# A one-core hybrid RWKV-7 layer: sample operands loaded at once into a free ring slot, group norm, bonus and state decay written with per-partition scalars

## The chip, the cores and the metric

The kernel runs on one NeuronCore of one Trainium2 chip, in fp32. The metric is device microseconds of one execution. Six engines matter here: PE (TensorE matmul) with its weight loads PEld, DVE (VectorE), ACT (ScalarE), POOL (GpSimd) and SP (SyncE), which here mostly issues DMAs; its queue is called SPq in the profile. The 16 DMA engines of the core move the data.

## The reference, cut to what matters

One decoder layer for 1024 prompt tokens and 64 sample tokens (8 sequences of 8 tokens). One input projection feeds an RWKV-7 time mix (8 heads of 64) and a sliding-window attention; both are gated, concatenated and projected, then a per-layer embedding gate and a last norm follow. The part that the change touches is the time mix and its output:

```
def step(S, inp):
    r_t, w_t, k_t, v_t, kk_t, a_t = inp
    sa = jnp.einsum('bhvk,bhk->bhv', S, kk_t)
    S = (S * w_t[:, :, None, :] - sa[..., None] * (kk_t * a_t)[:, :, None, :]
         + v_t[..., None] * k_t[:, :, None, :])
    return S, jnp.einsum('bhvk,bhk->bhv', S, r_t)
...
yn = (y - mean) * lax.rsqrt(var + GN_EPS) * ln_w.astype(f32).reshape(H, D) + ln_b.astype(f32).reshape(H, D)
bonus = jnp.sum(r * k * r_k.astype(f32).reshape(H, D), axis=-1, keepdims=True) * v
out = (yn + bonus).reshape(B, T, R).astype(z_shift.dtype)
```

It runs over the prompt with a zero state, and over the 8 sample sequences with the state that each brings along.

## The kernel before, in words

The time mix is computed in chunks of 64 tokens: chunks 0 to 15 are the prompt, chunk 16 is the sample. Four chunks form a unit, so units 0 to 3 are the prompt and unit 4 is the sample alone. For each unit `prepare` builds the Gram matrices of the chunk's keys and inverts a triangular matrix; the inversion is a long row of small DVE operations that alternate between two tiles, `tm` and `ti`, each needing the one before. Its result goes out to DRAM (`tt_d`) and comes back in another layout (`B`), is transposed on DVE (`t`) and finished by PE (`TE`, `TF`).

`steps` then carries the state from chunk to chunk. For each chunk, PE computes X1 from the state `sv` (L962), DVE copies it (L964, `rh`), PE computes X2 (L967), ACT and DVE negate it (L968, L969), PE computes X3 (L974), and DVE adds X3 to the decayed state to get the next chunk's `sv`. The decayed state `sg` = `sv` times GC is two POOL operations per chunk, made ahead. Afterwards the output Y of the chunk is made by PE (L987, L990) and normalised by DVE, ACT and POOL. `finish`, once per unit, multiplies each chunk's `y` by the inverse deviation `w` and the weight `lnw` (two POOL operations), multiplies the bonus value `bvl` by the bonus factor `bq` and adds it (two DVE operations), transposes on PE (L942, `ytr`) and stores.

`sample` is unit 4. Here the state differs by sequence, so PE needs the keys masked by sequence. For each head pair p it loads the two halves of the state (`s0`, shown as `s<-in_s0dup`, L1018, two DMAs of 128 KB) and the keys (`kd`, L1021, four DMAs), makes the masked keys `km` (one DVE and one POOL operation per key group), and runs 32 matmuls (L1029, `chS`). The four head pairs share five buffers of tag `y` and two of tag `kd`. DVE then copies `chS` (L1032, `rhS`), PE makes `csS` (L1039, L1044) with unit 4's `B`, and the sample's output is normalised and finished like a chunk.

The operand tiles of a prompt unit (L, two of them, K and B, each 128 partitions by 8 KB) live in two ring slots: slot 0 serves units 0 and 2, slot 1 units 1 and 3. The sample's own operands have a small third slot. Slot 0 is no longer needed once chunk 11, the last of unit 2, has made its Y.

The kernel is built under a tile scheduler: it estimates times and fixes from them the program order of each engine. So an edit also moves instructions that it does not name. Each engine runs its rows in that order; SP's order decides when a DMA can be issued. The stages are written down in a string, `"P0 P1 V0 S0 P2 S1 P3 S2 G4 H0 P4 X4 S3"` (P prepare, V first values, S steps, G gates, H output projection, X the sample). From about 450 us on, the other work that fills PE is the gate projections (`acc_gr`), the attention half of the output projection (`acc_wa`), then the RWKV half (`acc_wr`) and the per-layer gate (`acc_wg`, `pp`) with its row norms.

Of the kernel before, what the change touches and what calls it, by code (L numbers as in the profile page):

```python
# [739 lines left out]
def chain(e):  # L740
    nc, tc, A, O = e.nc, e.tc, e.A, e.O
    V, S, G, PE, SP = e.V, e.S, e.G, e.PE, e.SP
    tt, stt, ts, ps, pool, pc = e.tt, e.stt, e.ts, e.ps, e.pool, e.pc
    MUL, ADD, SUB, MAX = ALU.mult, ALU.add, ALU.subtract, ALU.max
    cst, par, ident, dp = e.cst, e.par, e.ident, e.dp
    kp = e.kp
    early = ("a2", "ti", "tm", "rn", "q2")
    tl = lambda shape, tag, name, bufs: (kp if tag in early else e.kp3 if tag in ("sv", "sg", "rh") else e.kp2).tile(
        shape, F32, tag=tag, name=name, bufs=bufs)
    LO, HI = slice(0, 64), slice(64, 128)  # L750

# [11 lines left out]
    ring = e.ring = {}  # L763
# [135 lines left out]
    def values(ch):  # L899

        q = tl([128, 4, 4, 64], "sv", f"sv{ch}", 2)
        for h, hs in enumerate((HI, LO)):
            DMAQ("sv").dma_start(q[hs, h::2], e.vt_d[ch % 2, ch // 2, h].unsqueeze(1).to_broadcast([64, 2, 4, 64]))
        return q

    def normalise(u, ci, ch, py, un):

        y = tl([128, 4, 64], "y", f"y{ch}", 5)
        mn = tl([128, 4], "mn", f"mn{ch}", 2)
        V.tensor_reduce(mn, py, AX, ADD)  # L910
        ts(G, mn, mn, 1.0 / 64, None, MUL)
        tt(V, y, py, mn.unsqueeze(2).to_broadcast([128, 4, 64]), SUB)
        q = tl([128, 4, 64], "yq", f"yq{ch}", 1)
        S.activation(q, y, AF.Square)
        V.tensor_reduce(un[:, ci], q, AX, ADD)
        return y

    def finish(u, ys, un):
        chs = units[u]
        n = len(chs)  # L920
        w = tl([128, 4, 4], "w", f"w{u}", 2)[:, :n]
        z = tl([128, 4, 4], "z", f"z{u}", 2)[:, :n]
        unv = un[:, :n]
        ts(V, unv, unv, 1.0 / 64, 64e-5, MUL, ADD)
        e.rsqrt(w, unv, z)
        bq = tl([128, 4, 4], "bq", f"bq{u}", 2)[:, :n]
        for b in range(2):
            nb = (n + 1 - b) // 2
            if nb:
                DMAQ("bq").dma_start(bq[:, b::2], e.bon_d[b, chs[0] // 2:chs[0] // 2 + nb].rearrange("c h t p -> (h t) c p"))  # L930
        for ci, ch in enumerate(chs):
            c, cl = src(ch)
            y = ys[ci]
            tt(G, y, y, w[:, ci].unsqueeze(2).to_broadcast([128, 4, 64]), MUL)
            tt(G, y, y, lnw, MUL)
            bv = tl([128, 4, 64], "bv", f"bvl{ch}", 2)
            DMAQ("bvl").dma_start(bv, e.vt_d[ch % 2, ch // 2].rearrange("h t p v -> (h t) p v"))
            tt(V, bv, bv, bq[:, ci].unsqueeze(2).to_broadcast([128, 4, 64]), MUL)
            tt(V, y, y, bv, ADD)
            t = ps("tr", f"ytr{ch}", 1)[:, 0:256].rearrange("p (a b) -> p a b", a=4)  # L940
            for q in range(2):
                PE.transpose(t[:, 2 * q:2 * q + 2].rearrange("p a b -> p (a b)"),  # L942
                             y[:, 2 * q:2 * q + 2].rearrange("p a b -> p (a b)"), ident)
            orr = tl([128, 4, 64], "or", f"or{ch}", 1)
            S.copy(orr, t)
            DMAQ("or").dma_start(e.or_d[c][:, :, 64 * cl:64 * cl + 64], orr)

    def steps(u, r, sv, last):
        chs = units[u]
        un = tl([128, 4, 4], "un", f"un{u}", 2)  # L950
        ys = []
        for ci, ch in enumerate(chs):
            L, K = r.L[ci], r.K[ci]
            pch = ps("ch", f"ch{ch}", 2).rearrange("p (a b) -> p a b", a=8)
            X1, X2 = pch[:, 0:4], pch[:, 4:8]
            sg = tl([128, 4, 64], "sg", f"sg{ch}", 2)
            for h, hs in enumerate((LO, HI)):
                tt(G, sg[hs], sv[hs, h], e.GC[hs, ch].unsqueeze(2).to_broadcast([64, 4, 64]), MUL)
            with tc.high_priority():
                for p in range(4):  # L960
                    for h, hs in enumerate((LO, HI)):
                        PE.matmul(X1[hs, p], L[h][:, p, 0:64], sv[:, h, p], start=True, stop=True)  # L962
                rh = tl([128, 4, 64], "rh", f"rh{ch}", 2)
                V.tensor_copy(rh, X1)  # L964
                for p in range(4):
                    for h, hs in enumerate((LO, HI)):
                        PE.matmul(X2[hs, p], r.B[hs, ci, p, 0:64], rh[hs, p], start=True, stop=True)  # L967
                S.activation(sv[LO, 2], X2[LO], AF.Copy, scale=-1.0)  # L968
                V.tensor_scalar(sv[HI, 3], X2[HI], -1.0, None, MUL)  # L969
                p3 = ps("ch", f"cs{ch}", 2).rearrange("p (a b) -> p a b", a=8)  # L970
                X3, Y = p3[:, 0:4], p3[:, 4:8]
                for p in range(4):
                    for h, hs in enumerate((LO, HI)):
                        PE.matmul(X3[hs, p], K[:, p, 64 * h:64 * h + 64], sv[:, 2 + h, p], start=True, stop=True)  # L974
                if ch < 15:
                    nx = values(ch + 1)
                    for h, hs in enumerate((LO, HI)):
                        tt(V, nx[hs, h], X3[hs], sg[hs], ADD)
                else:
                    so = tl([128, 4, 64], "rh", "so", 2)  # L980
                    tt(V, so, X3, sg, ADD)
                    SP.dma_start(O["wkvp"], so)
                    nx = None

            for p in range(4):
                for h, hs in enumerate((LO, HI)):
                    PE.matmul(Y[hs, p], L[h][:, p, 64:128], sv[:, h, p], start=p == 0, stop=False, skip_group_check=True)  # L987
            for p in range(4):
                for h, hs in enumerate((LO, HI)):
                    PE.matmul(Y[hs, p], r.B[hs, ci, p, 64:128], sv[hs, 2 + h, p], start=False, stop=True, skip_group_check=True)  # L990
            ys.append(normalise(u, ci, ch, Y, un))
            sv = nx
            e.fill(("s", u))
        finish(u, ys, un)
        return sv

    def sample(r):
        u, ch = 4, 16
# [3 lines left out]
        sv = tl([128, 2, 4, 64], "svS", "svS", 1)  # L1002
# [4 lines left out]
        mb = e.bm[:, :256].rearrange("p (b t) -> p b t", b=4)  # L1007
        for p in range(4):
            for q, dst in ((0, X1), (1, Y)):
                for h, hs in enumerate((LO, HI)):  # L1010
                    os_ = HI if h == 0 else LO
                    PE.matmul(dst[hs, p], L[h][os_, p, 64 * q:64 * q + 64], sv[os_, h, p], start=p + q == 0,
                              stop=False, skip_group_check=True)
        for p in range(4):
            s0, kd = [], []
            for h, hs in enumerate((LO, HI)):
                s0.append(tl([128, 4, 64], "y", f"s0{p}{h}", 5))
                DMAQ("s0").dma_start(s0[h], A["s0dup"][:, :, p, h])  # L1018
                kd.append(tl([128, 2, 64], "kd", f"kd{p}{h}", 2))
                for x in (LO, HI):  # L1020
                    DMAQ("s0").dma_start(kd[h][x], e.kq_d[16, hs, p].rearrange("k (s t) -> k s t", s=2))  # L1021
            for q, dst in ((0, X1), (1, Y)):
                km = []
                for h in range(2):
                    km.append(tl([128, 4, 64], "y", f"km{p}{h}{q}", 5))
                    tt(G if h else V, km[h], kd[h][:, q].unsqueeze(1).to_broadcast([128, 4, 64]), mb, MUL)
                for b in range(4):
                    for h, hs in enumerate((LO, HI)):
                        PE.matmul(dst[hs, p], km[h][:, b], s0[h][:, b], start=False, stop=b == 3, skip_group_check=True)  # L1029
            yield  # L1030
        rh = tl([128, 4, 64], "y", "rhS", 5)
        V.tensor_copy(rh, X1)  # L1032
# [13 lines left out]
        un = tl([128, 4, 4], "un", "unS", 2)  # L1046
        y = normalise(u, 0, ch, yy, un)
        finish(u, [y], un)
        yield
        b2 = e.bm[:, 256:].unsqueeze(2).to_broadcast([128, 8, 64])  # L1050
# [17 lines left out]
    for o in ORDER.split():  # L1068
        u = int(o[1])
        if o[0] == "V":  # L1070
            lnw = e.lnw = e.kp2.tile([128, 4, 64], F32, name="lnw")
# [4 lines left out]
            sv = values(0)  # L1076
# [11 lines left out]
        elif o[0] == "S":  # L1088
            sv = steps(u, rs[u], sv, 0)
# [414 lines left out]
```

## Time and profile before

| | |
|---|---|
| median of three runs | 960.12 us (959.53 to 960.18) |
| the profiled execution's own time | 954.67 us |
| its span, first to last instruction | 952.9 us |
| mean granted TensorE clock | 0.925 of full speed |
| PE busy | 837.2 us, 88% |
| PEld busy | 742.5 us, 78% |
| DVE busy | 640.8 us, 67%, 1511 instructions |
| ACT busy | 373.6 us, 39% |
| POOL busy | 371.8 us, 39%, 494 instructions |

The profiled execution is 5.45 us shorter than the median. Its span is what the trace's times count from; 1.8 us of the execution lie outside the span. Busy shares are averages over stages with different limits, so the table by windows of 50 us is the one to read. PEclk there is the granted clock as a share of full speed, and a busy PE at 0.70 does less than one at 1.00.

### The profile page before, as it was taken

To read this page: it belongs to the slowest core of one execution; us is meant where nothing else is said; L and a number is where in the kernel's file an instruction comes from. 1 tells how busy PE (TensorE), PEld (TensorE's weight loads), DVE (VectorE), ACT (ScalarE), POOL (GpSimd) and SP (SyncE) were. 2 spreads that over 40 slices of the span, in tenths; PEclk is the share of its full clock that TensorE was granted. 3 is DMA by queue.
4 is the path that set the end of the run, shared out by engine and by line. 5 is a ranking of instruction groups with operands and counts; after the bars stand their busy time and mean duration, and the time that the engine had idled before them with its cause. 6 is when DMAs were issued, how large, how long until landed. Compare 5 with 4: busy or idle time off the path is not lost.

```text
span 952.9 us, 17528 instructions
## 1 busy us (share of the span) xinstructions
PE 837.2 (88%) x6352; PEld 742.5 (78%) x6352; DVE 640.8 (67%) x1511; ACT 373.6 (39%) x864; POOL 371.8 (39%) x494
## 2 busy tenths in 40 slices
PE   6978999999999989898899875998893699999994
PEld 4878999788886779787788764887773588899993
DVE  7856487777777443388855778597963686864464
ACT  6202086666756432742233343313431144322131
POOL 7538466665667222323321333133442254301000
PEclk9989899999999999899899965998976799999997
DMA  8013201322226338546544597777657289998882
GB/s 288 23 64 96 65 23 56 101 91 71 69 90 176 84 83 220 162 104 164 149 131 132 139 306 231 179 259 188 204 171 230 69 280 334 335 308 289 267 295 99
DMA packets 151047, 157.81 MB, mean 166 GB/s; under 512 B 63688, under 2 KB 121288, under 8 KB 150824
## 3 DMA queue, kind: packets, MB, share of 16 engines
q1 hardware_dynamic: 150144, 155.57, 54.1%
q10 hardware_dynamic: 816, 1.11, 0.4%
q8 instruction: 50, 0.82, 0.4%
q14 instruction: 37, 0.30, 0.1%
HBM read 106.77 MB, written 49.67 MB: 164 GB/s over the span
## 4 chain that ended last, share of the span: by engine, by line
PE 40%; DVE 26%; DMA 15%; ACT 6%; issue 6%; SPq 4%; POOL 2%; DVEq 0%; ACTq 0%; POOLq 0%
PE acc_z L157 6%; PE acc_gr L157 4%; DVE tm L55 3%; PE acc_q L157 2%; DVE ti L55 2%; ACT s L425 2%; PE ov L446 2%; PE pp L1346 2%; DVE xl L58 2%; DMA a<-at_d 2%; PE acc_wg0g L157 1%; DMA sg<-sg_d 1%; DMA kd<-kq_d 1%; DMA L<-kq_d 1%; PE acc_wg4g L157 1%
## 5 line engine op out<-in xcount | busy, mean ns | idle before, releaser
L157 PE MATMUL acc_z<-xh,wh_z 128*128 128x384 f32 (+1 forms) x312 | 64.8, 339 | 0.0
L157 PE MATMUL acc_z<-xl,wh_z 128*128 128x384 f32 (+1 forms) x312 | 63.1, 333 | 0.0
L157 PE MATMUL acc_z<-xh,wl_z 128*128 128x384 f32 (+1 forms) x312 | 62.5, 331 | 0.0
L55 DVE TENSOR_TENSOR tm<-a,ti 128x56 f32<-128x56 f32 (+28 forms) x152 | 55.1, 362 | 3.6
L157 PEld LDWEIGHTS acc_z<-xh,wh_z 128*128 128x128 f32 x312 | 53.3, 190 | 1.7 <-ACT pTS L505 0.2
L157 PEld LDWEIGHTS acc_z<-xl,wh_z 128*128 128x128 f32 x312 | 53.1, 190 | 0.5
L157 PEld LDWEIGHTS acc_z<-xh,wl_z 128*128 128x128 f32 x312 | 52.3, 188 | 1.0 <-issue 0.2
L55 DVE TENSOR_TENSOR ti<-ti,tm 128x56 f32<-128x56 f32 (+28 forms) x152 | 48.1, 316 | 3.5
L55 POOL TENSOR_TENSOR sg<-sv,GC 64x256 f32<-64x256 f32 x32 | 21.5, 672 | 59.8 <-DVE sv L55 47.4
L64 POOL TENSOR_SCALAR s<-s,sm 128x256 f32<-128x256 f32 (+1 forms) x64 | 34.8, 560 | 17.2 <-ACT pT L444 4.6
L1185 ACT ACTIVATE q<-hx 128x384 f32<-128x384 f32 (+1 forms) x41 | 20.8, 507 | 48.8 <-DVE hx L58 20.8
L800 PE MATMUL gram<-L,K 64*128 64x128 f32 x272 | 31.6, 327 | 5.9 <-issue 4.0
L55 POOL TENSOR_TENSOR wl_z<-wr_z,wh_z 128x1024 fp32r<-128x1024 f32 x13 | 31.3, 2405 | 10.8 <-ACT wh_z L146 4.8
L800 PEld LDWEIGHTS gram<-L,K 64*128 64x128 f32 x272 | 27.0, 222 | 10.5 <-issue 7.5
L55 DVE TENSOR_TENSOR sq<-sq,q 128x384 f32<-128x384 f32 (+1 forms) x41 | 25.6, 624 | 13.1 <-ACT q L1185 12.4
L55 DVE TENSOR_TENSOR zr<-acc_z,R 128x384 f32<-128x384 f32 (+2 forms) x52 | 21.7, 433 | 18.5 <-PE acc_z L157 18.2
L425 ACT ACTIVATE s<-s,sm 128x256 f32<-128x256 f32 (+1 forms) x64 | 30.9, 485 | 1.9 <-DVE sm L62 1.9
L446 PE MATMUL ov<-pT,vtok 128*64 128x512 f32 x60 | 30.9, 633 | 0.4 <-ACT pT L444 0.4
L1356 ACT ACTIVATE t<-t 128x384 f32<-128x384 f32 (+3 forms) x25 | 12.2, 494 | 45.5 <-DVE t L55 45.4
L804 ACT COPY B<-L 64x512 f32<-64x512 f32 x34 | 20.9, 616 | 21.8 <-DVE L L55 20.9
L62 POOL TENSOR_SCALAR mn<-mn 128x4 f32<-128x4 f32 x17 | 4.4, 262 | 63.9 <-DVE mn L910 58.8
L55 DVE TENSOR_TENSOR L<-gram,cst 128x512 f32<-128x512 f32 x34 | 22.5, 684 | 8.7 <-PE gram L800 8.5
(620 smaller groups left out, 2458.4 us busy)
## 6 DMA issues: line engine op xcount, KB each, us to landing
wr_z<-in_wz SPq DMA_DIRECT2D x13, 512.0 KB
L<-kq_d SPq DMA_DIRECT2D x24, 256.0 KB
sv<-vt_d SPq DMA_DIRECT2D x32, 128.0 KB
wh_wo<-wo_dh SPq DMA_DIRECT2D x8, 512.0 KB
wl_wo<-wo_dl SPq DMA_DIRECT2D x8, 512.0 KB
raw<-in_xT SPq DMA_DIRECT2D x8, 384.0 KB
kq_d<-KQ SPq DMA_DIRECT2D x8, 384.0 KB
bk_d<-BK SPq DMA_DIRECT2D x8, 384.0 KB
```

The costliest lines, as they stand in the source:

```text
L55: e.tensor_tensor(out, a, b, op=op)
L58: V.scalar_tensor_tensor(out, a, s, b, op0, op1)
L62: e.tensor_scalar(out, a, s1, None, op0)
L64: e.tensor_scalar(out, a, s1, s2, op0, op1)
L157: PE.matmul(acc[:, :n], w_[:, k0 + k, :], a_[c][:, k, :n], start=i + k == 0, stop=i == 2 and k == K - 1)
L425: S.activation(s[:, j, :nk], s[:, j, :nk], AF.Exp, bias=m[:, 0, j:j + 1], accum_out=m[:, 2, j:j + 1])
L446: PE.matmul(ov[own, :], vtok[:, blk, own], pT[g].rearrange("p a b -> p (a b)"), start=pos == 0, stop=pos == nb - 1)
L800: PE.matmul(Gp[h][:, p], bk[hs, p], L[h][hs, p], start=True, stop=True)
L804: S.copy(r.B[hs, ci], L[h][hs])
L1185: e.S.square(q, h)
L1346: PE.matmul(pa, w[:, i], p[:, i], start=i + j == 0, stop=i == 1 and j == len(pr) - 1)
L1356: S.activation(t, t, AF.Tanh, scale=0.5)
```

## The change

Three edits. In `steps`, the two POOL operations for `sg` and the two DVE additions of 64 x 256 become eight DVE operations of 64 partitions x 64 elements that multiply the state by one GC value per partition and add X3 in the same pass. In `finish`, the two POOL and two DVE operations of 128 x 256 per chunk become eight DVE operations of 128 x 64: `y` times `w` times `lnw`, and `bv` times `bq` plus `y`. In `sample`, the state is one DMA of 1 MB into the first L tile of ring slot 0, the keys are four DMAs into the second, and all sixteen `km` are made at once in its K tile (DVE) and B tile (POOL), before one block of 128 `chS` matmuls.

```diff
-    tl = lambda shape, tag, name, bufs: (kp if tag in early else e.kp3 if tag in ("sv", "sg", "rh") else e.kp2).tile(
+    tl = lambda shape, tag, name, bufs: (kp if tag in early else e.kp3 if tag in ("sv", "rh") else e.kp2).tile(
...
-            tt(G, y, y, w[:, ci].unsqueeze(2).to_broadcast([128, 4, 64]), MUL)
-            tt(G, y, y, lnw, MUL)
             bv = tl([128, 4, 64], "bv", f"bvl{ch}", 2)
             DMAQ("bvl").dma_start(bv, e.vt_d[ch % 2, ch // 2].rearrange("h t p v -> (h t) p v"))
-            tt(V, bv, bv, bq[:, ci].unsqueeze(2).to_broadcast([128, 4, 64]), MUL)
-            tt(V, y, y, bv, ADD)
+            for p in range(4):
+                stt(y[:, p], y[:, p], w[:, ci, p:p + 1], lnw[:, p], MUL, MUL)
+            for p in range(4):
+                stt(y[:, p], bv[:, p], bq[:, ci, p:p + 1], y[:, p], MUL, ADD)
...
-            sg = tl([128, 4, 64], "sg", f"sg{ch}", 2)
-            for h, hs in enumerate((LO, HI)):
-                tt(G, sg[hs], sv[hs, h], e.GC[hs, ch].unsqueeze(2).to_broadcast([64, 4, 64]), MUL)
...
                 if ch < 15:
                     nx = values(ch + 1)
-                    for h, hs in enumerate((LO, HI)):
-                        tt(V, nx[hs, h], X3[hs], sg[hs], ADD)
+                    new = lambda h, hs: nx[hs, h]
                 else:
                     so = tl([128, 4, 64], "rh", "so", 2)
-                    tt(V, so, X3, sg, ADD)
+                    new = lambda h, hs: so[hs]
+                for p in range(4):
+                    for h, hs in enumerate((LO, HI)):
+                        stt(new(h, hs)[:, p], sv[hs, h, p], e.GC[hs, ch, p:p + 1], X3[hs, p], MUL, ADD)
+                if ch == 15:
                     SP.dma_start(O["wkvp"], so)
...
+        RS, RD, RM = ring[0][0], ring[0][1], ring[0][2:]
+        s0 = RS.rearrange("p c q d -> p (c q d)").rearrange("p (b q h v) -> p b q h v", b=4, q=4, h=2)
+        kd = RD.rearrange("p c q d -> p (c q d)")[:, :1024].rearrange("p (h q d) -> p h q d", h=2, q=4)
+        km = [x.rearrange("p c q d -> p (c q d)").rearrange("p (q s b t) -> p q s b t", q=4, s=2, b=4) for x in RM]
+        DMAQ("s0").dma_start(s0, A["s0dup"])
+        for h, hs in enumerate((LO, HI)):
+            for x in (LO, HI):
+                DMAQ("s0").dma_start(kd[x, h], e.kq_d[16, hs])
         for p in range(4):
-            s0, kd = [], []
-            for h, hs in enumerate((LO, HI)):
-                s0.append(tl([128, 4, 64], "y", f"s0{p}{h}", 5))
-                DMAQ("s0").dma_start(s0[h], A["s0dup"][:, :, p, h])
-                kd.append(tl([128, 2, 64], "kd", f"kd{p}{h}", 2))
-                for x in (LO, HI):
-                    DMAQ("s0").dma_start(kd[h][x], e.kq_d[16, hs, p].rearrange("k (s t) -> k s t", s=2))
+            for h in range(2):
+                for q in range(2):
+                    tt(G if h else V, km[h][:, p, q], kd[:, h, p, 64 * q:64 * q + 64].unsqueeze(1).to_broadcast([128, 4, 64]), mb, MUL)
+        for p in range(4):
             for q, dst in ((0, X1), (1, Y)):
-                km = []
-                for h in range(2):
-                    km.append(tl([128, 4, 64], "y", f"km{p}{h}{q}", 5))
-                    tt(G if h else V, km[h], kd[h][:, q].unsqueeze(1).to_broadcast([128, 4, 64]), mb, MUL)
                 for b in range(4):
                     for h, hs in enumerate((LO, HI)):
-                        PE.matmul(dst[hs, p], km[h][:, b], s0[h][:, b], start=False, stop=b == 3, skip_group_check=True)
+                        PE.matmul(dst[hs, p], km[h][:, p, q, b], s0[:, b, p, h], start=False, stop=b == 3, skip_group_check=True)
```

The scheduler moves more than the diff shows. SP's queue before, around the second and third head pair's loads (`s<-in_s0dup` is the state, `kd` the keys; the other rows are stores and weights):

```order
357 L1018 DMA s_7021<-in_s0dup 128x4x64
358 L946 DMA or_d_3665<-or_5973 512x1x64
359 L1021 DMA kd_7023<-kq_d 64x128 x2
360 L1021 DMA kd_7028<-kq_d 64x128
361 L1018 DMA s_7026<-in_s0dup 128x4x64
362 L1021 DMA kd_7028<-kq_d 64x128
363 L1302 DMA wg_dl<-wl_wg1g_8176 128x1024
364 L1152 DMA or_8050<-or_d_3665 128x768
365 L1153 DMA sg_8051<-sg_d_3659 128x768
```

And SP's queue now, around the one load of the state (L1019, into the L tile `L_3687`; `sv_7252` are the values of chunk 13):

```order
336 L1304 DMA wo_dl<-wl_wor6c_8040 128x2x512
337 L1272 DMA wl_wor0c_8154<-wo_dl 128x2x512
338 L143 DMA wr_wg1g_8239<-in_wg 128x1024
339 L1019 DMA L_3687<-in_s0dup 128x2048
340 L903 DMA sv_7252<-vt_d 64x2x256 x2
341 L1304 DMA wg_dh<-wh_wg0g_8178 128x1024
```

The sample's loads no longer lie between the stores of unit 2's outputs and the weights of the gate stage; the state's load stands ahead of the values of chunk 13, and the keys' loads 13 to 30 rows ahead of it.

DVE before, near the end of unit 4's triangular inversion (`ti_6869`, `tm_6874`), with the next state `sv` of chunk 14 and the additions of unit 2's outputs `y`:

```order
1083 L55 TENSOR_TENSOR ti_6869<-ti_6869,tm_6874 64x2x3
1084 L55 TENSOR_TENSOR y_5717<-y_5717,bvl_5930 128x256
1085 L55 TENSOR_TENSOR tm_6874<-a_4_6853,ti_6869 64x4
1086 L55 TENSOR_TENSOR sq_7832<-sq_7832,q_7993 128x384
1087 L55 TENSOR_TENSOR ti_6869<-ti_6869,tm_6874 64x4
1088 L58 SCALAR_TENSOR_TENSOR ul_7831<-hx_6823,par,uh_7830 128x384
1089 L55 TENSOR_TENSOR y_5779<-y_5779,bvl_5942 128x256
1090 L55 TENSOR_TENSOR hx_6823<-acc_wr7c_0_7998,hx_6823 128x384
1091 L55 TENSOR_TENSOR sv_7280<-cs_7271,sg_7248 64x256 x2
```

The same stretch of DVE now (`ti_6953`, `tm_6958` are the inversion's tiles, `rhS` the copy of the sample's `chS`, `rsv` and `rsy` a row norm):

```order
1111 L55 TENSOR_TENSOR ti_6953<-ti_6953,tm_6958 64x2x3
1112 L1034 COPY rhS<-chS 128x256
1113 L64 TENSOR_SCALAR rsv_8084<-st_8083 128x3
1114 L55 TENSOR_TENSOR tm_6958<-a_4_6937,ti_6953 64x4
1115 L58 SCALAR_TENSOR_TENSOR y_5906<-bvl_6028,bq_5993,y_5906 128x64 x4
1116 L62 TENSOR_SCALAR rsy_8085<-rsv_8084 128x3
1117 L55 TENSOR_TENSOR ti_6953<-ti_6953,tm_6958 64x4
1118 L58 SCALAR_TENSOR_TENSOR y_5971<-bvl_6044,bq_5993,y_5971 128x64 x4
1119 L55 TENSOR_TENSOR tm_6958<-a_4_6937,ti_6953 64x7
1120 L64 TENSOR_SCALAR rsy_8085<-rsy_8085 128x3
1121 L55 TENSOR_TENSOR ti_6953<-ti_6953,tm_6958 64x7
1122 L55 TENSOR_TENSOR rsq_8086<-rsy_8085 128x3
```

The inversion of unit 4 used to end ahead of everything that reads the sample's `chS`; now its last rows stand behind `rhS`, most of those behind the new `sv` of chunk 14 as well (row 1123, eight operations), and the last `ti` is row 1144. On PE the 128 matmuls of `chS` now stand as one block, after chunk 12's X3 and before `acc_wg0g`, with X1 and X2 of chunk 13 among them; before, they were spread from `acc_wg0g` to `csS`.

## Rows read from the trace of the kernel before

**Rows 1.** Windows of 50 us: length, busy of each engine, granted clock, DMA share, GB/s.

```profile
550.00:600.00 50.00, 33.98 (x260) 29.31 (x261) 40.73 (x109) 20.29 (x45) 18.31 (x26) 0.65 0.87 258
600.00:650.00 50.00, 45.83 (x532) 41.12 (x530) 39.26 (x104) 13.73 (x23) 12.51 (x14) 0.97 0.77 227
650.00:700.00 50.00, 41.03 (x515) 34.74 (x515) 44.43 (x129) 18.49 (x35) 24.78 (x23) 0.84 0.63 187
700.00:750.00 50.00, 30.78 (x333) 24.97 (x332) 24.89 (x61) 9.31 (x21) 13.78 (x18) 0.70 0.54 162
...
800.00:850.00 50.00, 49.29 (x287) 44.43 (x284) 38.40 (x89) 15.80 (x33) 13.52 (x13) 1.00 0.95 323
```

**Rows 2.** Groups of instructions by line, 450 to 760 us: busy, mean ns, idle before.

```profile
L1029 PE MATMUL chS<-s,km 128*64 128x64 f32 x128 | 8.9, 276 | 13.3 <-DVE km L55 9.7 <-POOL km L55 3.5
```

**Rows 3.** Timeline of PE, 681 to 755 us: start, length, what, idle before and releaser.

```profile
681.07 0.68 PE L990 MATMUL cs<-sv,B 64*64 64x64 f32 x16
...
698.07 2.91 PE L157 MATMUL acc_wg0g<-uh,wh_wg0g 128*128 128x384 f32 x8
...
732.05 1.70 PE L1029 MATMUL chS<-s,km 128*64 128x64 f32 x18 [4.41 <-DVE km L55]
...
736.20 1.21 PE L1039 MATMUL csS<-rhS,B 64*64 64x64 f32 x16 [0.68 <-DVE rhS L1032]
...
741.75 1.12 PE L962 MATMUL ch<-sv,L 128*64 128x64 f32 x16 [2.28 <-DVE y L55]
...
754.20 0.97 PE L157 MATMUL acc_wr0c<-mrh,wh_wor0c 128*128 128x384 f32 x4
```

**Rows 4.** The chain that ended last, 700 to 745 us, in order of time.

```profile
714.19 6.76 DMA wh_wor2c<-wo_dh
...
724.75 6.00 DMA kd<-kq_d
```

**Rows 5.** Timeline of DVE: end of unit 4's inversion, and its return from DRAM.

```profile
691.63 0.15 DVE L55 TENSOR_TENSOR ti<-ti,tm 64x4 f32<-64x4 f32 x1
...
701.81 0.30 DVE L879 STREAM_TRANSPOSE t<-B 32x128 f32<-32x128 f32 x1 [0.76 <-DMA B<-tt_d]
```

**Rows 6.** Instructions of tile sg: ns min/median/max, first and last start.

```profile
L55 POOL TENSOR_TENSOR sg<-sv,GC x32: 605/610/1671, 459.1 to 748.5; 64x256 f32<-64x256 f32 x32
L55 DVE TENSOR_TENSOR sv<-cs,sg x30: 404/422/429, 479.8 to 747.6; 64x256 f32<-64x256 f32 x30
```

**Rows 7.** Tile zsr: an existing form with a per-partition scalar, down to 128x64.

```profile
L58 DVE SCALAR_TENSOR_TENSOR zsr<-zr,par,zsr x16: 272/559/1256, 149.7 to 285.0; 128x384 f32<-128x384 f32 x8, 128x256 f32<-128x256 f32 x4, 128x64 f32<-128x64 f32 x4
```

**Rows 8.** Timeline of DVE, 279 and 683 us: independent operations that follow each other.

```profile
279.15 0.21 DVE L55 TENSOR_TENSOR zr<-acc_z,R 128x64 f32<-128x64 f32 x1
279.29 0.69 DVE L58 SCALAR_TENSOR_TENSOR zsr<-zr,par,zsr 128x384 f32<-128x384 f32 x1
...
683.17 0.15 DVE L55 TENSOR_TENSOR tm<-a,ti 64x4 f32<-64x4 f32 x1
683.24 0.16 DVE L58 SCALAR_TENSOR_TENSOR z<-z,un 128x16 f32<-128x16 f32 x1
```

**Rows 9.** Instructions of tile y, columns as in rows 6.

```profile
L55 POOL TENSOR_TENSOR y<-y,w x17: 608/613/1060, 529.5 to 770.4; 128x256 f32<-128x256 f32 x17
L55 POOL TENSOR_TENSOR y<-y,lnw x17: 721/727/2460, 531.8 to 775.8; 128x256 f32<-128x256 f32 x17
L55 DVE TENSOR_TENSOR y<-y,bvl x17: 407/418/949, 532.6 to 781.4; 128x256 f32<-128x256 f32 x17
```

**Rows 10.** Timelines of DVE and POOL, 583 to 589 us: the inversion of unit 2.

```profile
583.48 0.23 DVE L55 TENSOR_TENSOR tm<-a,ti 128x70 f32<-128x70 f32 x1
583.74 0.56 DVE L55 TENSOR_TENSOR ti<-ti,tm 128x70 f32<-128x70 f32 x1
...
588.05 0.63 DVE L55 TENSOR_TENSOR tm<-a,ti 128x16 f32<-128x16 f32 x1
...
583.61 2.33 POOL L55 TENSOR_TENSOR y<-y,w 128x256 f32<-128x256 f32 x4 [7.53 <-DVE w L58]
```

## The prediction

> **What bounds the kernel now.** The windows of 50 us come first [rows 1]. PE is the bound at 800 to 850 us (49.3 of 50 us busy at full clock), but not from 550 to 750 us: there it idles 16.0, 4.2, 9.0 and 19.2 us, and its clock is low in the first window (0.65) and the last (0.70). The last is the weakest stretch of this half of the kernel: DVE has only 24.9 us of work in it, POOL 13.8, and the DMA share is 0.54. So nothing is full; things wait for each other. The groups of instructions say what [rows 2]: the 128 `chS` matmuls of the sample work 8.9 us and PE stands 13.3 us in front of them, for `km` on DVE and POOL. The timeline of PE gives the places [rows 3], such as 4.41 us before 732.05. Behind the last `chS` come `csS` at 736.20, X1 of chunk 14 at 741.75 and only at 754.20 `acc_wr0c`, the first large work in which PE is full again. The chain that ended last shows why `km` is late [rows 4]: it goes through a load of keys, of 32 KB, that needs 6.00 us to land, behind a weight load of 512 KB that needs 6.76 us; each is issued when a shared buffer comes free. The sample's loads are therefore a chain of buffers and DMA round trips, on the path that sets the end.
>
> **The change, part by part.**
>
> **The sample's loads.** Eight state loads and sixteen key loads become one and four, and sixteen `km` can be made as soon as the keys are there, which SP issues well ahead. The wait of 13.3 us for `km` [rows 2] goes. What is late next is the state: its slot is free when chunk 11 has made Y, which ended at 681.75 us [rows 3]. The trace has no load of 1 MB. The nearest rows are 6.00 us (32 KB) and 6.76 us (512 KB) [rows 4]: lower bound 6, upper bound twice the second, 13.5. These two differ little for sixteen times the bytes, so I take 8. With about 2 us of lateness of chunk 11 (below) and 1 us to issue, the state lands at about 693. Then 128 matmuls, at 0.07 us each as in the row of 18 in 1.70 us, or 9 us at the low clock [rows 3], with some of chunk 13's between: the block ends near 702 instead of 735.
>
> **What stands behind the block.** `acc_wg0g`, 698.07 us before [rows 3], now follows it, at about 702, and ends near 707 with chunk 13's X3 behind. On DVE, unit 4's inversion, which ended at 691.63 before [rows 5], now ends behind `rhS` and the new `sv` of chunk 14, so near 711: this is the new late one. From its last `ti` to the transpose `t` it takes 10.2 us (691.63 to 701.81 [rows 5]), two DMA trips that the change leaves alone: `t` at about 721, covered on PE by `acc_wg1g` and `pp`. `TE` and `TF` I put at 2.5 us, an estimate from the 1 us that 16 to 18 small matmuls take [rows 3], twice, and a copy; then `csS` at 724. From `csS` to X1 of chunk 14 took 5.55 us (736.20 to 741.75 [rows 3]); it comes at 729.6, so 12.1 us earlier.
>
> **State decay.** 32 POOL operations of 0.61 us (median) go, 21 us in all with the longer ones; none was waited for at the chunk step, so POOL's relief is worth nothing by itself [rows 6]. On DVE two additions of 0.42 us become eight operations of 64 elements. The nearest form in the trace, with a per-partition scalar and 128 x 64, takes 0.272 us at the least [rows 7]; that is the upper bound of what each costs in a row: 2.2 us. The lower is the pitch of independent operations of 4 elements: 683.17 to 683.24, 0.07 us, so 0.7 us [rows 8]. One of 128 x 64 with duration 0.21 lets the next start after 0.14 (279.15 to 279.29): an overlap of 0.07. I take 0.272 less 0.07, so 0.20, and 1.7 us for eight: plus 0.85 us per chunk, 14 us over 16 chunks (bounds minus 2 and plus 22). It lies directly on the chain from chunk to chunk.
>
> **Group norm and bonus.** Two DVE operations of 0.42 us become eight of 0.20: plus 0.85 us per chunk, 14.5 us over 17 chunks (bounds minus 2.5 and plus 23). Two POOL operations of 0.61 and 0.73 us per chunk go, 23 us [rows 9]. There is a gain in them on DVE: beside POOL's `y` of unit 1, from 583.61 us on, `ti` and `tm` take 0.56 to 0.63 us where the one before takes 0.23 [rows 10]. Nine operations run there, at about 0.35 us each: 3.2 us, which nearly pays for that unit's 3.4 us. The same holds beside unit 2's four chunks.
>
> A rule of the Trainium skill stands against both edits. In "VectorE: DVE Perf Modes", section "The TRN2 errata — SBUF-src ops pay a fixed extra latency per instruction", it says that a vector operation pays a fixed latency, so that many small tiles pay it many times, and it advises tiles of 512 elements or more. By its measured fixed term of about 150 cycles an operation of 64 elements is estimated at 0.22 us, and the two edits together at 31 us of DVE work instead of my 28.5. For the old additions of 256 elements the same term would give 0.42 us, and the row agrees (418 ns [rows 9]). No run here shows the new forms yet.
>
> **Sum.** From 550 us to chunk 11's Y: four state updates and unit 1's finish cost 3.4 us each, less the 3.2 us of stall; most of the rest lies in DVE's idle time (25.6 of the 150 us from 550 to 700 are idle [rows 1]) or under the `acc_wa` matmuls. I take plus 2, the lateness used above. To X1 of chunk 14: minus 12.1, with that in it. One more state update to chunk 15, plus 0.85, and `acc_wr0c` comes 11.2 us earlier, at 743. Behind it the finishes of unit 3 and the sample add 5 x 0.85 = 4.3 us on DVE, less a stall of some 1.5, partly under PE's work: plus 2. The rest, in which PE is full, moves as it is: **minus 9 us**. Against the profiled execution of 954.67 us that gives 945.7. The median of the runs stands 5.45 us above that execution, so the forecast in its terms is **951 us**.
>
> **The rivals.**
> *Unit 4's inversion does not hold back.* If DVE reaches its last rows as early as PE allows, `csS` follows `acc_wg1g` directly, at about 716, and the clock stays up in the block: 8 us more, 943. For it: DVE had 25 us of idle time in that stretch. Against: the order puts the last `ti` behind `sv`, which waits for X3 behind `acc_wg0g`.
> *The edit does not free the loads.* The one load is all or nothing: if it takes the 13.5 us of the upper bound, PE stands in front of the block, with nothing of the queue behind it movable ahead, and 5.5 us are lost; chunk 13's values and the stores of `wg_dh` are queued behind it on SP. With the DMA engines at 0.95 in 800 to 850 us [rows 1], weights that now are wanted earlier may not come earlier and take the rest: 958 to 961, no change.
> *VectorE becomes the bound* (the other side). The mechanism: no overlap between the small operations, so plus 1.4 us per update and per finish, in line in the chunk chain and in the inversions of units 2 and 4. From chunk 4 to 15 that is 12 updates and 8 finishes, 28 us, less 7 of stalls; against the 25.6 us of idle time, which is scattered, I reckon that all 21 come through, less the 12 won at the sample: 969 us, plus 9. It decides where the price of an operation passes 0.25 us or where the inversion, not PE, ends last in each unit. That is also where the skill's rule points. For it: PE idles 16 us in 550 to 600 us, when DVE is busiest (40.7). Against: the stalls that POOL causes there go with the same edit.
>
> **How the numbers follow.** Forecast 0.52 (947 to 956); inversion early 0.15; loads not freed 0.14; VectorE bound 0.19. A measurement of this kernel can tell about 0.2%, here 1.9 us. Faster by over 0.2%: all of the first two but 0.02, and 0.05 of the third: 0.70. Within: 0.02 of the first and 0.08 of the third, and 0.02 of the fourth: 0.12. Slower: 0.17 of the fourth and 0.01 of the third: 0.18. The range reaches from the early inversion to the middle of the cases of a loss: 940 to 965.
>
> **What would show it.** In the profile after: `chS` as one stretch with no wait for `km`, and one wait of 1 to 5 us for the DMA of the state before it; `acc_wg0g` at about 702, X1 of chunk 14 at about 730, `acc_wr0c` at about 743; rows of 64 x 64 and 128 x 64 on DVE with eight in about 1.7 us; `ti` and `tm` of unit 2 without the 0.5 us durations around finish; POOL busy some 45 us less, DVE 10 to 20 us more; PEclk of the 700 to 750 window above 0.70. Wrong would be: the small operations at 0.28 us each in a row; chunk 8's steps more than 4 us later than before; the state landing after 697; a wait of PE for `TE` that ends after 725; or DMA waits in 760 to 840 us that take back what the sample won.

## The result and the profile after

The change makes the kernel **slower**: 969.95 us (968.62 to 974.23, four runs) against 959.83 us (four runs) for the kernel before, a ratio of 1.0118 with a 95% interval of 1.0082 to 1.0154. The forecast was 951 us. Of all the executions behind this document one, of 985.62 us (e10), fell in a slower state of the chip, and the ratios leave it out.

| | before | after |
|---|---|---|
| median of the runs | 959.83 us | 969.95 us |
| the profiled execution | 954.67 us | 974.23 us |
| its span | 952.9 us | 972.4 us |
| DVE busy | 640.8 us, x1511 | 664.0 us, x1710 |
| POOL busy | 371.8 us, x494 | 326.4 us, x428 |

One caution holds for the whole of what follows: the profiled execution before lies 5.2 us under its median and the one after 4.3 us over it, so the two traces differ by 19.6 us where the runs differ by 10.1. Places are read from the traces, sizes from the runs. In one place the trace shows where its execution lost time: from 500 to 513 us PE is busy throughout, but the granted clock is 0.51 of full speed, the lower of its two levels (1.2 of 2.4 GHz). X2 of chunk 2, 16 matmuls, takes 1.12 us there. In the kernel before it takes 0.68 us, at a clock of 1.00. In the 8 us up to 496, before its clock fell, PE had been busy 6.97 us. The windows, with the columns of [rows 1], are first that of the changed kernel and then that of the kernel before:

```profile
500.00:513.00 13.00, 13.00 (x146) 11.02 (x148) 3.05 (x7) 2.38 (x5) 0.22 (x1) 0.51 0.27 63
```

```profile
494.00:504.00 10.00, 10.00 (x173) 8.76 (x174) 4.33 (x10) 3.11 (x7) 2.03 (x4) 1.00 0.57 165
```

The page of the changed kernel, its part 1:

```profile
PE 850.8 (87%) x6352; PEld 754.5 (78%) x6352; DVE 664.0 (68%) x1710; ACT 374.0 (38%) x864; POOL 326.4 (34%) x428
```

POOL lost 45 us, as forecast, and DVE gained 23 us (forecast 10 to 20). The windows after, with the columns of [rows 1]:

```profile
550.00:600.00 50.00, 35.02 (x326) 27.03 (x325) 43.08 (x143) 17.09 (x39) 7.56 (x8) 0.74 0.94 273
600.00:650.00 50.00, 46.03 (x451) 41.73 (x451) 36.96 (x107) 17.02 (x31) 12.21 (x13) 0.88 0.77 224
650.00:700.00 50.00, 40.54 (x499) 34.71 (x498) 44.12 (x116) 18.54 (x33) 19.89 (x20) 0.93 0.72 227
700.00:750.00 50.00, 32.54 (x412) 27.76 (x412) 34.19 (x142) 11.35 (x25) 5.77 (x6) 0.74 0.48 149
750.00:800.00 50.00, 37.02 (x260) 33.65 (x261) 39.45 (x112) 14.28 (x29) 11.62 (x10) 0.75 0.57 190
```

The last of these windows in the kernel before, for comparison:

```profile
750.00:800.00 50.00, 43.42 (x280) 38.19 (x279) 36.61 (x64) 19.89 (x38) 22.25 (x20) 0.94 0.76 253
```

The weak stretch of 700 to 750 us has not gone; a second one, 750 to 800 us at 0.75 of full clock (0.94 before), stands behind it. The next fence is the groups of instructions from 450 to 780 us, as in [rows 2]:

```profile
L58 DVE SCALAR_TENSOR_TENSOR sv<-sv,GC,cs 64x64 f32<-64x64 f32 x120 | 33.6, 280 | 5.4 <-PE cs L971 2.0
...
L58 DVE SCALAR_TENSOR_TENSOR y<-bvl,bq,y 128x64 f32<-128x64 f32 x52 | 12.8, 287 | 0.5 <-DMA bvl<-vt_d 0.4
L58 DVE SCALAR_TENSOR_TENSOR y<-y,w,lnw 128x64 f32<-128x64 f32 x52 | 11.9, 281 | 0.0
...
L1031 PE MATMUL chS<-L,K 128*64 128x64 f32 x64 | 6.2, 266 | 0.0
L1031 PE MATMUL chS<-L,B 128*64 128x64 f32 x64 | 6.2, 266 | 0.0
```

The sample's edit does what it says: the 128 `chS` matmuls now wait for nothing (0.0 where 13.3 us stood). What is late is ahead of them and behind them. The timeline of PE after, answering to [rows 3]; the first row is Y of chunk 11, the second chunk 12's X2, the third chunk 12's X3 just ahead of the block, the last two X1 of chunk 14 and the first `acc_wr0c` behind it:

```profile
694.05 0.68 PE L990 MATMUL cs<-sv,B 64*64 64x64 f32 x16
...
696.91 0.68 PE L964 MATMUL ch<-rh,B 64*64 64x64 f32 x16 [1.23 <-DVE rh L961]
701.64 0.45 PE L971 MATMUL cs<-sv,K 128*64 128x64 f32 x2 [3.16 <-DVE ti L55]
...
738.53 0.97 PE L1041 MATMUL csS<-rhS,B 64*64 64x64 f32 x16 [0.37 <-ACT B L894]
...
748.29 1.12 PE L959 MATMUL ch<-sv,L 128*64 128x64 f32 x16 [7.18 <-DVE y L55]
...
766.37 1.65 PE L157 MATMUL acc_wr0c<-mrh,wh_wor0c 128*128 128x384 f32 x4
```

Which row of the kernel before answers to the first has to be counted, since the rows carry no chunk numbers. X3 of chunk 15 is the last at 753.58 us, and counted back from it these are X3 of chunk 11, Y of chunk 11 and X3 of chunk 12:

```profile
658.74 0.48 PE L974 MATMUL cs<-sv,K 128*64 128x64 f32 x2
...
666.65 0.68 PE L990 MATMUL cs<-sv,B 64*64 64x64 f32 x16
...
673.87 0.69 PE L974 MATMUL cs<-sv,K 128*64 128x64 f32 x16
```

So the Y at 681.07 in [rows 3] is that of chunk 12, and chunk 11's Y, at 694.05 us, comes 27.4 us later than before. The lateness came in steps: X3 is 1.6 us late in chunk 1, 10.8 in chunk 2 (the stretch at the low clock, where X1 of chunk 2 is also spread over 7.3 us between other matmuls, against 2.9 before), 11.1 in chunk 7, 20.1 in chunk 8, behind unit 2's inversion, and 27.3 in chunk 11. The timeline of DVE has the end of unit 4's inversion and its return, answering to [rows 5]:

```profile
725.15 0.15 DVE L55 TENSOR_TENSOR ti<-ti,tm 64x4 f32<-64x4 f32 x1
...
732.89 0.30 DVE L879 STREAM_TRANSPOSE t<-B 32x128 f32<-32x128 f32 x1 [1.38 <-DMA B<-tt_d]
```

The inversion ends 33.5 us later than before, and with it `B`, the last thing that `csS` waits for. One more wait follows, on DVE again:

```profile
744.01 1.15 DVE L58 SCALAR_TENSOR_TENSOR or<-or,lnb,sg 128x384 f32<-128x384 f32 x2 [2.43 <-DMA sg<-sg_d]
745.07 0.41 DVE L910 TENSOR_REDUCE mn<-yS 128x4 f32<-128x256 f32 x1
```

A row of the output projection that waits for a DMA stands on DVE ahead of the normalisation; X1 of chunk 14, whose row names the normalisation's `y`, comes 9.8 us after `csS` where it was 5.55.

### The profile page after: what moved, and what is told of

Same layout as the page of the kernel before. It is cut to its first block, busy times and chain, and to the rows that moved or that the text cites. A ratio compares the mean times of both kernels' runs of the same rounds, so it can differ in the third digit from the quotient of the medians.

```text
span 972.4 us, 17568 instructions
## 1 busy us (share of the span) xinstructions
PE 850.8 (87%) x6352; PEld 754.5 (78%) x6352; DVE 664.0 (68%) x1710; ACT 374.0 (38%) x864; POOL 326.4 (34%) x428
## 4 chain that ended last, share of the span: by engine, by line
PE 43%; DVE 26%; DMA 12%; issue 7%; ACT 7%; SPq 3%; POOL 2%; DVEq 0%; ACTq 0%; POOLq 0%
PE acc_z L157 6%; DVE tm L55 3%; PE acc_gr L157 3%; PE acc_wa L157 2%; DVE ti L55 2%; PE acc_q L157 2%; PE pp L1348 2%; ACT s L425 2%; DVE y L58 2%; PE ov L446 2%; PE acc_wg3g L157 2%; DVE sv L58 2%; PE acc_wg0g L157 1%; PE acc_wg7g L157 1%; PE acc_wg5g L157 1%
## 5 line engine op out<-in xcount | busy, mean ns | idle before, releaser
L55 DVE TENSOR_TENSOR tm<-a,ti 128x56 f32<-128x56 f32 (+28 forms) x152 | 52.9, 348 | 2.9
L58 DVE SCALAR_TENSOR_TENSOR sv<-sv,GC,cs 64x64 f32<-64x64 f32 x120 | 33.6, 280 | 5.4 <-PE cs L971 2.0
L959 PE MATMUL ch<-sv,L 128*64 128x64 f32 x256 | 22.3, 261 | 12.8 <-DVE y L55 7.2
L959 PEld LDWEIGHTS ch<-sv,L 128*64 128x64 f32 x256 | 16.6, 159 | 20.2 <-DVE y L55 7.3
```

The lines of the kernel that those rows point to most:

```text
L55: e.tensor_tensor(out, a, b, op=op)
L58: V.scalar_tensor_tensor(out, a, s, b, op0, op1)
```

## The experiments

Two theories for the loss were set against each other, with a third against both. A: the state decay costs the time, in the chain from chunk to chunk. B: the norm's small operations cost it, in the inversions. C: the sample's block costs it. The three edits were taken apart and recombined. "Ratio" is to the kernel before on the same chip, with a 95% interval.

**e1, the sample alone.** The change without its edits of `steps` and `finish`:

```diff
+            sg = tl([128, 4, 64], "sg", f"sg{ch}", 2)
+            for h, hs in enumerate((LO, HI)):
+                tt(G, sg[hs], sv[hs, h], e.GC[hs, ch].unsqueeze(2).to_broadcast([64, 4, 64]), MUL)
...
-                for p in range(4):
-                    for h, hs in enumerate((LO, HI)):
-                        stt(new(h, hs)[:, p], sv[hs, h, p], e.GC[hs, ch, p:p + 1], X3[hs, p], MUL, ADD)
...
-            for p in range(4):
-                stt(y[:, p], y[:, p], w[:, ci, p:p + 1], lnw[:, p], MUL, MUL)
+            tt(G, y, y, w[:, ci].unsqueeze(2).to_broadcast([128, 4, 64]), MUL)
...
```

> Only the sample's loads are changed; state decay and group norm are as before. Theory A (the state decay in eight small operations costs the time: 2.46 us for eight in the changed kernel's trace against 0.87 for two, in the chain from chunk to chunk) and theory B (the group norm's small operations among the inversion's cost it): the gain of the sample stands alone, 942 to 952 us, chunk 11 as early as before, chunk 14's X1 10 us or more earlier than before. Theory C (the one block and its load cost the time): 960 us or more.

Measured: 941.44 us, 0.9828 (0.9793 to 0.9862), just under the range of A and B. C falls. The timelines of PE and DVE of e1:

```profile
696.96 0.32 PE L1041 MATMUL csS<-rhS,B 64*64 64x64 f32 x2 [0.57 <-ACT B L894]
...
710.81 0.69 PE L962 MATMUL ch<-sv,L 128*64 128x64 f32 x16
...
682.84 0.15 DVE L55 TENSOR_TENSOR ti<-ti,tm 64x4 f32<-64x4 f32 x1
```

X1 of chunk 14 stands 31 us earlier than before; since the scheduler put `acc_wr7c` to `acc_wg1g` behind it, about 14 us of that reach the end of the trace.

**e2, the state decay put back**, the norm and the sample as changed (the first two hunks of e1).

> The changed kernel with the state decay put back (POOL multiplies, two additions on DVE). Theory A: 944 to 955 us, the lateness of 27 us at chunk 11 falls below 10. Theory B: 962 to 970 us, lateness at chunk 11 of 15 us or more remains.

Measured: 942.34 us, 0.9825 (0.9775 to 0.9874). That is 2 us under A's range and far from B's; chunk 11's X3 is 7.5 us late in the trace, as A had it:

```profile
666.27 0.69 PE L974 MATMUL cs<-sv,K 128*64 128x64 f32 x16 [0.75 <-DVE sv L969]
```

**e3, the norm put back**, the state decay and the sample as changed (the last hunk of e1).

> The changed kernel with group norm and bonus put back on POOL and DVE. Theory A: 963 to 972 us, lateness at chunk 11 of 15 us or more. Theory B: 944 to 957 us, lateness at chunk 11 below 10.

Measured: 955.61 us, 0.9979 (0.9945 to 1.0013), chunk 11's X3 16.0 us late:

```profile
674.79 0.33 PE L971 MATMUL cs<-sv,K 128*64 128x64 f32 x2
```

The lateness is what A expected; the time is 7 us under A's range and within B's. So the decay costs 14 us beside the sample's gain (e3 against e1), and is not all of the loss.

**e4, the state decay alone**, in the kernel before.

> The kernel before with the state decay alone changed. Theory A: 972 to 985 us, since its 1.6 us per chunk and what follows from it come without the sample's gain. Theory B: 958 to 965 us.

Measured: 969.39 us, 1.0112 (1.0067 to 1.0157): plus 12 us, a little under A's range and clear of B's.

**e8, the norm alone**, in the kernel before.

> The kernel before with group norm and bonus alone changed. If the norm's small operations cost nothing by themselves, as e1 against e2 has it: 954 to 961 us. If they cost time wherever unit 2's and unit 4's inversions end last, which e2's sample gain may hide: 963 to 970 us.

Measured: 968.51 us, 1.0105 (1.0076 to 1.0134): plus 11 us. Beside the sample's change (e1 against e2) the same edit had shown nothing. The groups of DVE in unit 2's inversion, before (551 to 589 us, 37 us long):

```profile
L55 DVE TENSOR_TENSOR tm<-a,ti 128x126 f32<-128x126 f32 (+22 forms) x31 | 12.5, 402 | 0.6
L55 DVE TENSOR_TENSOR ti<-ti,tm 128x126 f32<-128x126 f32 (+22 forms) x31 | 12.2, 393 | 0.7
L55 DVE TENSOR_TENSOR L<-gram,cst 128x512 f32<-128x512 f32 x4 | 2.8, 688 | 0.1
```

and in e8 (551.4 to 599.7 us, 48 us long):

```profile
L55 DVE TENSOR_TENSOR ti<-ti,tm 128x126 f32<-128x126 f32 (+22 forms) x31 | 11.2, 360 | 0.5
L55 DVE TENSOR_TENSOR tm<-a,ti 128x126 f32<-128x126 f32 (+22 forms) x31 | 10.1, 325 | 0.5
L55 DVE TENSOR_TENSOR L<-gram,cst 128x512 f32<-128x512 f32 x10 | 6.8, 687 | 2.7 <-PE gram L800 2.6
L58 DVE SCALAR_TENSOR_TENSOR y<-y,w,lnw 128x64 f32<-128x64 f32 x16 | 4.6, 326 | 0.0
L58 DVE SCALAR_TENSOR_TENSOR y<-bvl,bq,y 128x64 f32<-128x64 f32 x8 | 2.0, 274 | 0.0
```

The inversion's own 62 operations got 3.4 us shorter, near the forecast's 3.2 for the stalls beside POOL. But it ends 11 us later: 6.6 us of the norm stand in it, six more copies of Gram matrices of 4.0 us, and 2.6 us of a wait for PE. These copies are work that the scheduler moved here, so the norm's own operations are only part of the 11 us. That the later inversion is what costs the kernel 11 us is a reading of the trace; no run takes it out alone.

**e10, state decay and norm together**, the sample as before.

> The kernel before with state decay and norm both changed and the sample as before. If the two add up (plus 12 and plus 11 measured alone): 976 to 985 us. If they hide behind each other, since both lie in the same stretches of DVE: 968 to 974 us.

Measured: 975.29 us as the median of 970.38, 975.29 and 982.1 us (978.70 with the fourth run), and a ratio of 1.0243 (1.0187 to 1.0298). That is plus 19 us by the median and plus 23 by the ratio, against 12 and 11 alone: nearer to adding up than to hiding, with the size open by 4 us.

**e5, the order of the eight small operations.** As e3, with the two loops exchanged:

```diff
-                for p in range(4):
-                    for h, hs in enumerate((LO, HI)):
+                for h, hs in enumerate((LO, HI)):
+                    for p in range(4):
                         stt(new(h, hs)[:, p], sv[hs, h, p], e.GC[hs, ch, p:p + 1], X3[hs, p], MUL, ADD)
```

> As e3 (sample and state decay changed), but the eight small operations do the four pairs of the lower 64 partitions first, then the four of the upper. Theory D (the step of 0.31 us from one to the next comes from alternating between the halves): the eight take 1.8 us or less, and the time falls from 955.6 to 946 to 951 us. Theory E (it comes from the PSUM operand or the operation itself): they take 2.4 us still, and the time stays at 952 to 959 us.

Measured: 950.93 us, 0.9924 (0.9894 to 0.9954). D holds for the step, clearly. The time lies at the upper end of D's range, and its interval just touches that of e3 (0.9945 to 1.0013), so the gain in time is likely but not clear of noise. The timelines of DVE, e3 first, then e5, then a row of the kernel before:

```profile
525.14 2.46 DVE L58 SCALAR_TENSOR_TENSOR sv<-sv,GC,cs 64x64 f32<-64x64 f32 x8 [0.31 <-PE cs L971]
```

```profile
520.29 1.76 DVE L58 SCALAR_TENSOR_TENSOR sv<-sv,GC,cs 64x64 f32<-64x64 f32 x8 [0.18 <-PE cs L971]
```

```profile
493.50 0.87 DVE L55 TENSOR_TENSOR sv<-cs,sg 64x256 f32<-64x256 f32 x2
```

Eight operations of 0.28 us take 2.46 us when lower and upper partitions alternate, a step of 0.31 from one to the next, and 1.76 us, a step of 0.21, when they do not. The old pair of 0.42 us each took 0.87: it alternates too, and does not overlap either.

**e6 and e7, ahead or in the chain.** Both start from e1. e6 makes the decayed state on DVE, ahead; e7 lengthens the chain behind each state addition:

```diff
-                tt(G, sg[hs], sv[hs, h], e.GC[hs, ch].unsqueeze(2).to_broadcast([64, 4, 64]), MUL)
+                tt(V, sg[hs], sv[hs, h], e.GC[hs, ch].unsqueeze(2).to_broadcast([64, 4, 64]), MUL)
```

```diff
                         tt(V, nx[hs, h], X3[hs], sg[hs], ADD)
+                    for h, hs in enumerate((LO, HI)):
+                        for _ in range(2):
+                            V.tensor_scalar(nx[hs, h], nx[hs, h], 1.0, None, MUL)
```

> As e1 (sample alone changed), but the multiplication for the decayed state runs on DVE, ahead, in place of POOL: two more DVE operations of 64x256 per chunk, and the two additions in the chain as before. Theory F (what counts is the price between X3 and the next chunk's X1): 940 to 946 us, like e1. Theory G (what counts is DVE's load): 949 to 957 us.

> As e1, but behind each state addition four more DVE operations of 64x256 that multiply the new state by one, in place: about 1.7 us more between X3 and the next X1 of each chunk, and nothing else; the decay stays on POOL. Theory F: the time rises to 950 to 958 us, as much as the small operations cost in e3. Theory H (the small operations cost time because they let the scheduler take X1 apart and put other matmuls between): 941 to 947 us.

Measured: e6 946.88 us, 0.9878 (0.9851 to 0.9906); e7 960.20 us, 1.0026 (1.0001 to 1.0051). The rows are 0.87 us per pair ahead in e6 and 1.25 us for the four in e7, less than the 1.7 expected:

```profile
493.77 0.87 DVE L55 TENSOR_TENSOR sg<-sv,GC 64x256 f32<-64x256 f32 x2
```

```profile
495.44 1.25 DVE L981 TENSOR_SCALAR sv<-sv 64x256 f32<-64x256 f32 x4
```

Over 16 chunks e6 adds 14 us of DVE work ahead of the chain and costs 5; e7 adds some 19 us in the chain (15 chunks of 1.25) and costs 19. F and G are each half right: in this pair work beside the chain comes through to a third or so, work in the chain nearly whole. It is no rule, since the 25 us that the dearer decay adds to the chain came through to 14 in e3. H falls as the only cause: a longer chain alone costs time. It is not excluded as a part, and how much of e7's cost is the scheduler's other order cannot be told.

**e9, the whole change with e5's order of loops.**

> The whole change, with the eight small operations of the state decay in the order of e5 (four pairs of the lower 64 partitions, then four of the upper). If the price in the chain from chunk to chunk is the cause (2.46 us falls to 1.76): 0.7 us less per chunk, 11 us over 16, of which e3 against e5 let 0.4 through, so 958 to 966 us, and chunk 11 some 5 to 10 us earlier than in the changed kernel. If the cause is the norm's operations in the inversions alone: 967 to 973 us, as the change.

Measured: 956.21 us, 0.9998 (0.9970 to 1.0026). Each ratio is to the kernel before on its own chip, and by them (0.9998 against 1.0118) e9 is 11 to 12 us better than the change, as much as the whole price of 11 us. The groups of its unit 2 inversion (551.4 to 586.8 us) show that more than the price changed:

```profile
L58 DVE SCALAR_TENSOR_TENSOR sv<-sv,GC,cs 64x64 f32<-64x64 f32 x16 | 3.5, 279 | 0.0
L55 DVE TENSOR_TENSOR L<-gram,cst 128x512 f32<-128x512 f32 x4 | 2.7, 685 | 0.0
```

The scheduler, given the other order, put none of the norm's operations in it, and it is 35 us long. The two effects are not separated.

**e11, the norm's small operations for unit 3 and the sample only**, in e1 (`if u >= 3` ahead of them, the old four operations otherwise).

> As e1 (sample changed, state decay as before), and the norm's small operations for unit 3 and the sample only, whose finish runs beside no inversion. If the norm costs time only where an inversion waits among it: 937 to 943 us, no worse than e1 (941.4). If eight small operations cost as much anywhere: 943 to 947 us.

Measured: 946.16 us, 0.9875 (0.9839 to 0.9910), against e1's 0.9828: in the upper range. By the ratios that is some 4.5 us for five chunks outside the inversions, though the intervals overlap. It speaks against the idea that only the inversion makes them dear, but does not settle it: e2, with the same operations in all 17 chunks, stood at 0.9825, no worse than e1, so the 4.5 us may be the scheduler's order.

The table puts the three edits together (ratios):

| | sample as before | sample changed |
|---|---|---|
| decay and norm as before | 1 | 0.9828 (e1) |
| norm changed | 1.0105 (e8) | 0.9825 (e2) |
| decay changed | 1.0112 (e4) | 0.9979 (e3) |
| both changed | 1.0243 (e10) | 1.0118 (the change) |

e1 beats both kernels, by 16 us and 28 us.

## Why the prediction was wrong

**The sample's loads: right in mechanism and sign, its size too small.** Forecast minus 12 at X1 of chunk 14 and minus 9 in the end; alone it is worth minus 16 us (e1). One reason is a misread row: "its slot is free when chunk 11 has made Y, which ended at 681.75 us [rows 3]" takes chunk 12's Y for chunk 11's, which ended at 667.3 us, so the sum lets the load start 14 us too late. "What is late next is the state" did not come: in the changed kernel its load was issued at 694.1 us and `chS` began at 703.5 with no wait for it; in e1 the two lie 6.2 us apart (665.1 and 671.3), so the load lands in 6.2 us or less where I took 8 (the changed kernel's rows, then e1's):

```profile
694.05 0.35 SPq L1019 DMA_DIRECT2D L<-in_s0dup  x1
703.52 0.31 PE L1031 MATMUL chS<-L,K 128*64 128x64 f32 x1
```

```profile
665.07 0.34 SPq L1019 DMA_DIRECT2D L<-in_s0dup  x1
671.28 0.27 PE L1031 MATMUL chS<-L,K 128*64 128x64 f32 x1
```

"`t` at about 721" came at 732.9 in the changed kernel and at 688.9 in e1. The trip from the last `ti` to `t`, taken as 10.2 us, was shorter in both (7.7 and 6.0 us); what was wrong is the end of the inversion, 725.15 us in the changed kernel where I took 711. And "0.07 us each as in the row of 18 in 1.70 us" is not what that row says: 1.70 us over 18 is 0.09. The figure fits the row of 16 in 1.12 us [rows 3], and the block took 6.9 us against the 9 taken.

**State decay: the price of one operation was wrong.** "I take 0.272 less 0.07, so 0.20, and 1.7 us for eight" was worked out from operations on the same partitions [rows 8]. The new ones alternate between halves and step at 0.31: 2.46 us, plus 1.6 us per chunk and 25 us over 16 instead of 14. The range had a step of 0.272 as its upper bound, so the measured price lay outside it. The right row was there: the pair of old additions, which alternates the same way, takes 0.87 us for two of 0.42. e5 shows that the order is the cause, with 1.76 us, which is the forecast's figure.

**Norm and bonus: price right, place wrong.** Its operations step at 0.20 us as taken:

```profile
595.16 0.47 DVE L58 SCALAR_TENSOR_TENSOR y<-y,w,lnw 128x64 f32<-128x64 f32 x2
595.55 0.28 DVE L58 SCALAR_TENSOR_TENSOR y<-bvl,bq,y 128x64 f32<-128x64 f32 x1
```

(two in 0.47 us, the next one 0.39 after the first). The gain from POOL's absence was right too, though the long operations from 583.74 to 588.05 us [rows 10] are eight and not nine. Yet e8 costs 11 us.

**The step that failed for both** is "most of the rest lies in DVE's idle time (25.6 of the 150 us from 550 to 700 are idle [rows 1])" and with it "I take plus 2". Chunk 11 was not 2 us late but 27 in the changed kernel's trace, and 7.5 to 16 in those of e2, e3, e4, e8 and e10, which hold one or both of the edits; in e1, which holds neither, its X3 is 1.1 us late. The idle time is not in the inversion: its 62 operations have 1.3 us of it before them in unit 2 (the groups before, under e8). There each operation needs the one before it, so what is put between pushes the rest back. In the changed kernel, four operations of the norm stand between a `ti` and the `tm` that needs it:

```profile
594.01 0.27 DVE L55 TENSOR_TENSOR ti<-ti,tm 128x110 f32<-128x110 f32 x1
594.20 0.87 DVE L58 SCALAR_TENSOR_TENSOR y<-y,w,lnw 128x64 f32<-128x64 f32 x4
594.98 0.26 DVE L55 TENSOR_TENSOR tm<-a,ti 128x108 f32<-128x108 f32 x1
```

The `tm` starts 0.97 us after the `ti`, where operations of this size with nothing between start 0.31 us apart: 0.66 us more, of the 0.8 that four steps take. The sum also starts "From 550 us" and gives the seven state updates before that nothing, without a reason. X3 of chunk 6, the last before 550 us, was 15.9 us late in the changed kernel's trace, and 6.1 in e4 and 3.4 in e3, which have the same decay. The difference is about what the changed kernel's trace lost in the stretch at the low clock; whether its other executions lose it too is not known.

Alone the two edits cost 12 and 11 us, together 19 to 23 (e4, e8, e10); against the sample's 16 that leaves plus 3 to 7. Measured is plus 10, so 3 to 7 us are not the sum of the parts; the wait behind `or<-or,lnb,sg` would be of that size, but no run isolates it.

**The rivals.** "VectorE becomes the bound" is what came. Its decision point, a price over 0.25 us or an inversion that ends last in its unit, was right; 969 us was the time it gave, against 970 measured. It was given 0.19. Its mechanism, no overlap between the small operations, holds for the decay only, and the sample's gain that it took off was 12 where e1 gives 16. So that the two numbers agree is in part luck. "Unit 4's inversion does not hold back", 943 us, is near what the sample alone gives (941), but not by its path: in e1 `csS` comes at 696.96, ahead of `acc_wg1g` and not behind it. "The edit does not free the loads" falls.

The rule of the Trainium skill ("VectorE: DVE Perf Modes", "The TRN2 errata — SBUF-src ops pay a fixed extra latency per instruction") spoke against both edits, and e4 and e8 are slower, as its advice has it. The estimate of 0.22 us by its fixed term is close to the step of the norm's operations, 0.20, and of e5's decay, 0.21. It is less than their recorded duration of 0.28 and than the step of 0.31 for alternating halves, and there the measurement decides.

**What stays open.** The norm costs 11 us alone and nothing beside the sample's change (e2 against e1), but 13 us, by the ratios, when the decay is there too (e3 against the change). In e2's trace it delays the chunks all the same: X3 is 9.5 us later than in e1's in chunk 8 and 9.2 in chunk 13, but the span only 4.3. Lateness of the chunks does not reach the end whole. Each recombination also gave the scheduler another order, in e9 plainly so, and no run holds the order still.

## What to carry to other kernels

Price a small operation from a row in which the same kind of operands follow each other, on the same partitions and in the same order, not from any pair that overlaps. On an in-order engine ask where in the queue the added work will stand: in a chain of dependent operations it costs most of its step, whatever share of the window the engine idles. A bundle of edits should be taken apart: here one of three was worth minus 16 us, and the other two, without it, cost 19 to 23.

## What the runs showed of the hardware that was not expected

Eight independent VectorE operations of 64 partitions x 64 elements take 2.46 us when they alternate between the lower and the upper 64 partitions and 1.76 us when four of one half come before four of the other, with 0.28 us for each in both cases. And a load of 1 MB (128 partitions x 8 KB) landed within 6.2 us, where one of 32 KB took 6.00 us and one of 512 KB 6.76 [rows 4].
